# First two weight pairs of the down projection on the POOL queue, first pair's sums in the row ring

## The chip, the cores and the metric

One core of a Trainium2 chip. The metric is the device time of one execution in microseconds, median of several runs. TensorE (PE) multiplies, VectorE (DVE) and ScalarE (ACT) work on rows in SBUF and empty TensorE's banks, POOL (GpSimd) and SP (SyncE) here mainly issue DMAs, each on a queue of its own.

## The reference

One layer of a hybrid decoder on 1024 prompt tokens, 32 sample tokens and 16 meta tokens, in fp32: a norm, an input projection, a gated short convolution beside retention, an output projection, a second norm and a SwiGLU FFN. What matters here is its end:

```python
x = x + jnp.concatenate([conv_out, ret_out], axis=-1) @ w_out
xn = _rmsnorm(x, norm2_g)
x = x + (jax.nn.silu(xn @ w_gate) * (xn @ w_up)) @ w_down
...
y_prompt = _rmsnorm(xp, final_norm_g)[:, N_META:]
y_sample = _rmsnorm(xs, final_norm_g)
```

`w_gate` and `w_up` are 1024 x 2816, `w_down` is 2816 x 1024. A layer's `x` before the FFN is called `x1` below.

## The kernel before

**Numbers.** Every fp32 operand is split into two parts of a type that TensorE takes at full rate: hi (ScalarE, L153 for weights, L786 for FFN results) and lo = operand - hi (VectorE, L155, L787). Each product is made of three passes: hi by hi, hi by lo, lo by hi.

**Strassen.** The FFN's products and the down projection use a Strassen-Winograd scheme (`strassen`, L746) over 2 x 2 blocks: seven products instead of eight, in the order y1, z1, y2, w1, y3, z2, y4, into three PSUM banks `y`, `z` and `u` (names with the prefix "b" in the FFN, "d" in the down projection: `dy`, `dz`, `dw`). Four weight blocks a11, a21, a22, a12 are loaded into `wraw` (five buffers, `load_w`, L146, on SP's queue). Four sums of weights, s3 = a11 + a21, s1 = a21 + a22, s2 = s1 + a11, s4 = s2 + a12, are formed on VectorE (L750, names `s`); y1 needs a11 alone, z1 needs s3, y2 needs s2, w1 a12, y3 s1, z2 a22, y4 s4. After each product `on(step, ps)` is called, which reads the bank; y2, y3 and y4 go on adding in the bank of y1, so each has to wait until `on` has read what stood there.

**FFN.** A loop over 22 tiles of 128 hidden columns (`f`). Its right operands, the normed rows in seven Strassen combinations, are the 56 tiles `comb`. They lie in the pool `rows`: one ring of 62 buffers of 128 x 544 that serves nearly every row of the kernel (`ut`, L130). The FFN's other tiles (`gt`, `up`, sums of weights, ...) lie in the pool `late`. The result of a tile, `up`, is sent to DRAM (`hd`, and `hp` for the last four tiles) as hi and lo by the spill of the next tile, by POOL's queue (L788, L789). In the last tile (`f == NFF - 1`) the first rows `x1` (4 buffers) and the 28 tiles of block 0 are pulled back from DRAM into the ring (`pull`, L831, on SP's queue), four after each product.

**Down projection.** `late` is closed (L918) and the pool `fin` opened in its place. The hidden rows are taken in four blocks (`DBLOCKS`, `bi`), and per block in four pairs of output rows (`m` = 0, 2, 4, 6; called pair 0, 2, 4, 6), each one a `strassen` call with sums of weights in `fin` (two buffers of `ws`). Pair 0 of block 0 has its `x1` rows in the ring; for pairs 2, 4 and 6 four rows each are loaded into `fin` in block 0 (L948). `on` adds the bank to the `x1` row (L954) and pulls the next block's tiles, one after each product in block 0, so seven a pair:

```python
for m in range(0, KT, 2):
    ...                                   # four load_w of w_down
    if bi == 0 and m > 0:
        ...                               # four loads of x1 (L948)
    def on(step, ps):
        ...
        V.tensor_tensor(x, x, ps, ALU.subtract if i else ALU.add)   # L954
        advance(ahead, step_n)
    strassen(fin, a11, a21, a22, a12, w, nk, dn_rhs, "d", on)
```

**Order.** The order of the instructions on an engine or queue is not quite that of the text. The framework runs the program through a timing of its own: what is ready and has its buffers goes, and among what is ready what stands earlier in the text goes first. Then each engine runs its list strictly in that order. So an instruction that waits holds up all behind it on its engine.

## Time and profile before

| What | Value |
|---|---|
| Median of 3 runs | 1222.28 us (1221.14 to 1223.32) |
| The profiled execution | 1221.89 us, span of its instructions 1220.0 us |
| Granted clock of TensorE, mean | 0.992 |
| PE busy | 1196.4 us (98%) |
| DVE busy | 845.1 us (69%) |
| ACT busy | 486.3 us (40%) |
| POOL busy | 122.3 us (10%) |
| DMA | 163.02 MB, mean 134 GB/s |

The profile lists instructions by line, engine and operation, with names of tiles (`out<-in`). All matmuls of the FFN and the down projection have line 762, so products are told apart by their banks. `hb` and `ht` are pulled tiles of hidden rows, `hd` and `hp` their place in DRAM, `x1d` that of the rows `x1`, `by`, `bz`, `bw` the banks of the FFN, `dy`, `dz`, `dw` those of the down projection. PE is matmuls, PEld the weight loads beside them; SPq and POOLq are DMA issues on those queues. Times in the traces are microseconds from the start of the span; the last FFN tile runs from about 942.3 to 962.6.

### The profile page before, as it was taken

The numbers are of one execution on the slowest core, as the hardware profiler recorded it, in microseconds if no ns is written. First come the engines' busy times: TensorE is split into PE (matmuls) and PEld (weight loads), VectorE is DVE, ScalarE is ACT, GpSimd is POOL, SyncE is SP. The second block draws the span as 40 slices with busy tenths as digits, with TensorE's granted clock in tenths as the row PEclk, the third lists the DMA queues.
The fourth block names the chain that finished last, engine by engine and source line by source line (L and its number), as shares of the span: only waits on it lengthen the run. The fifth ranks groups of instructions, "written<-read, shape, count | busy, mean of one in ns | idle before, by whom it ended". The sixth has DMA issues, their size and how long they took to land.

```text
span 1220.0 us, 24549 instructions
## 1 busy us (share of the span) xinstructions
PE 1196.4 (98%) x9769; PEld 1183.3 (97%) x9769; DVE 845.1 (69%) x1592; ACT 486.3 (40%) x932; POOL 122.3 (10%) x251
## 2 busy tenths in 40 slices
PE   8999999999999999999999999999999899999996
PEld 8999988999999999999999999999999899999996
DVE  5455466676554577868777877787776588886665
ACT  8246531121223366644444444444343322222353
POOL 0100121000000012102201220222021100000000
PEclk9999998999999999999999999999999999999998
DMA  6321311100111255525424542544353998964213
GB/s 232 96 81 35 87 36 44 36 27 27 48 37 53 89 171 183 168 77 176 159 81 169 177 148 82 177 150 156 101 186 114 396 348 286 314 221 161 74 38 106
DMA packets 82066, 163.02 MB, mean 134 GB/s; under 512 B 10701, under 2 KB 23776, under 8 KB 81952
## 3 DMA queue, kind: packets, MB, share of 16 engines
q1 hardware_dynamic: 67568, 114.57, 29.1%
q0 software_dynamic: 14384, 46.89, 10.6%
q8 instruction: 77, 1.26, 0.4%
q14 instruction: 37, 0.30, 0.1%
HBM read 113.15 MB, written 48.26 MB: 132 GB/s over the span
## 4 chain that ended last, share of the span: by engine, by line
PE 80%; issue 10%; DVE 4%; DMA 3%; POOL 2%; ACT 1%; SPq 0%; DVEq 0%; POOLq 0%; ACTq 0%
PE by L762 14%; PE dy L762 8%; PE bz L762 7%; PE po L180 6%; PE pk L180 4%; PE dz L762 4%; PE pc L180 4%; PE pd L995 4%; PE pv L180 4%; PE pq L180 4%; PE pg L180 4%; PE bw L762 3%; PE pb L180 3%; PE ph L180 3%; PE dw L762 2%
## 5 line engine op out<-in xcount | busy, mean ns | idle before, releaser
L153 ACT ACTIVATE whi<-wraw 128x512 fp32r<-128x512 f32 (+2 forms) x198 | 115.6, 584 | 289.9 <-issue 62.8
L155 DVE TENSOR_TENSOR wlo<-wraw,whi 128x512 fp32r<-128x512 f32 (+2 forms) x198 | 124.4, 629 | 56.4 <-ACT whi L153 56.3
L153 ACT ACTIVATE whi<-s 128x512 fp32r<-128x512 f32 (+2 forms) x152 | 83.6, 551 | 162.7 <-PE by L762 49.7
L762 PE MATMUL by<-t,whi 128*128 128x256 f32 (+1 forms) x704 | 131.1, 285 | 0.0
L762 PE MATMUL bz<-t,whi 128*128 128x256 f32 (+1 forms) x704 | 131.0, 285 | 0.0
L762 PE MATMUL by<-b,whi 128*128 128x256 f32 (+1 forms) x704 | 129.9, 284 | 0.6 <-DVE up L890 0.6
L155 DVE TENSOR_TENSOR wlo<-s,whi 128x512 fp32r<-128x512 f32 (+2 forms) x152 | 89.4, 588 | 36.2 <-ACT whi L153 35.8
L762 PEld LDWEIGHTS by<-b,whi 128*128 128x128 f32 x704 | 109.3, 188 | 1.0 <-DVE up L890 1.0
L762 PEld LDWEIGHTS by<-t,whi 128*128 128x128 f32 x704 | 109.4, 188 | 0.0
L762 PEld LDWEIGHTS bz<-t,whi 128*128 128x128 f32 x704 | 109.4, 188 | 0.0
L762 PE MATMUL by<-t,wlo 128*128 128x256 f32 (+1 forms) x352 | 100.2, 285 | 0.0
L762 PE MATMUL by<-b,wlo 128*128 128x256 f32 (+1 forms) x352 | 100.2, 285 | 0.0
L762 PE MATMUL bz<-t,wlo 128*128 128x256 f32 (+1 forms) x352 | 100.2, 285 | 0.0
L762 PEld LDWEIGHTS by<-t,wlo 128*128 128x128 f32 x352 | 66.6, 189 | 0.0
L762 PEld LDWEIGHTS bz<-t,wlo 128*128 128x128 f32 x352 | 66.3, 188 | 0.0
L762 PEld LDWEIGHTS by<-b,wlo 128*128 128x128 f32 x352 | 66.1, 188 | 0.0
L762 PE MATMUL bw<-b,whi 128*128 128x272 f32 (+1 forms) x352 | 65.6, 285 | 0.0
L954 DVE TENSOR_TENSOR x<-x,dy 128x528 f32<-128x528 f32 x64 | 45.0, 704 | 25.9 <-PE dy L762 24.9
L788 POOL DMA_DIRECT2D hd<-hh x63 | 34.1, 542 | 277.8 <-ACT hh L786 275.7
L762 PE MATMUL dz<-ht,whi 128*128 128x256 f32 (+1 forms) x288 | 55.1, 288 | 3.6 <-ACT whi L153 3.6
L762 PE MATMUL dy<-hb,whi 128*128 128x256 f32 (+1 forms) x288 | 53.3, 284 | 1.7 <-ACT whi L153 1.7
L762 PEld LDWEIGHTS bw<-b,whi 128*128 128x128 f32 x352 | 54.5, 188 | 0.0
(303 smaller groups left out, 3200.5 us busy)
## 6 DMA issues: line engine op xcount, KB each, us to landing
ht<-hd SPq DMA_DIRECT2D x72, 264.0 KB, 5.1
hd<-hh POOLq DMA_DIRECT2D x63, 264.0 KB, 3.4
hd<-hl POOLq DMA_DIRECT2D x63, 264.0 KB, 3.7
hb<-hd SPq DMA_DIRECT2D x54, 264.0 KB, 5.1
wraw<-w_in SPq DMA_DIRECT2D x54, 256.0 KB, 2.8
wraw<-w_gate SPq DMA_DIRECT2D x44, 256.0 KB, 2.9
wraw<-w_up SPq DMA_DIRECT2D x44, 256.0 KB, 2.8
wraw<-w_out SPq DMA_DIRECT2D x32, 256.0 KB, 3.0
```

Of the source, the lines that this page charges most:

```text
L153: S.activation(hi[:, :n], raw[:, :n], AF.Copy)
L155: V.tensor_tensor(lo[:, :n], raw[:, :n], hi.bitcast(F32)[:, :n], ALU.subtract)
L180: T.matmul(ps[:, g, :n], wt[:, sl], xk[part][:, g * n:(g + 1) * n], start=(first and i == 0), stop=(last and i == 2))
L762: T.matmul(out, wt[:, sl], rhs(s, k, key, part), start=(first and k == 0 and i == 0), stop=(k == kt - 1 and i == 2), skip_group_check=not ...
L788: G.dma_start(dst[0], hi.bitcast(F32)[:, :HT])
L954: V.tensor_tensor(x, x, ps, ALU.subtract if i else ALU.add)
L995: T.matmul(ps[:, 0, :n], wt[:, sl], hs[k][g][part][:, SO[s]:SO[s] + n], start=(k == 0 and i == 0), stop=(k == NPL - 1 and i == 2))
```

## The change

- `load_w` takes the engine whose queue issues the load. A new function `down_w` makes the four loads of a pair.
- Pair 0 of block 0: its four loads are issued on POOL's queue, and stand in the text in the last FFN tile, after its product z2. Pair 2 of block 0: its four loads stay where they were and go to POOL's queue. All others stay on SP's queue.
- The four sums of weights of pair 0 of block 0 are tiles of the ring `rows` and not of `fin`.

```diff
-        def load_w(ap, n):
+        def load_w(ap, n, eng=D):
             raw = wts.tile([P, 512], F32, tag="wraw", name="wraw", bufs=5)
-            D.dma_start(raw[:, :n], ap)
+            eng.dma_start(raw[:, :n], ap)
             return raw
...
             def total(nm, a, b):
-                x = pool.tile([P, 512], F32, tag="ws", name=nm, bufs=4 if n > 384 else 2)
+                if pool is rows:
+                    x = ut(nm)
+                else:
+                    x = pool.tile([P, 512], F32, tag="ws", name=nm, bufs=4 if n > 384 else 2)
                 V.tensor_tensor(x[:, :n], a[:, :n], b[:, :n], ALU.add)
                 return x
...
+        def down_w(bi, m, eng=D):
+            p0, p1 = DBLOCKS[bi]
+            w, at = (p1 - p0) * P, 2 * p0 * P
+            return [load_w(t["w_down"][m + i][:, a:a + w], w, eng)
+                    for i, a in ((0, at), (1, at), (1, at + w), (0, at + w))]
+
+        down_first = []
...
+                if f == NFF - 1 and step == "z2":
+                    down_first.extend(down_w(0, 0, G))
                 if f == 0 and step in ("y2", "w1"):
...
             for m in range(0, KT, 2):
                 w = nk * P
-                at = 2 * p0 * P
-                a11, a21 = (load_w(t["w_down"][m + i][:, at:at + w], w) for i in range(2))
-                a22, a12 = (load_w(t["w_down"][m + i][:, at + w:at + 2 * w], w) for i in (1, 0))
+                if bi == 0 and m == 0:
+                    a11, a21, a22, a12 = down_first
+                else:
+                    a11, a21, a22, a12 = down_w(bi, m, G if bi == 0 and m == 2 else D)
...
-                strassen(fin, a11, a21, a22, a12, w, nk, dn_rhs, "d", on)
+                strassen(rows if bi == 0 and m == 0 else fin, a11, a21, a22, a12, w, nk, dn_rhs, "d", on)
```

## The prediction

> **What bounds the kernel now.** I read the page's busy times, then the waits of TensorE, then the chain of waits and the timelines around the change, then the DMA queues there. First the page and the two waits of TensorE that lie in this place:

> ```profile
> PE 1196.4 (98%) x9769; PEld 1183.3 (97%) x9769; DVE 845.1 (69%) x1592; ACT 486.3 (40%) x932; POOL 122.3 (10%) x251
> PE dz L762 <- ACT whi L153: 3.6, 1, 3.6
> PE dy L762 <- ACT whi L153: 1.7, 1, 1.7
> ```

> TensorE is the bound: time is saved where it stands still or runs slowly, and lost only where it stands. Both waits are at the start of the down projection. From the view of stretches (columns: length; busy time of PE, PEld, DVE, ACT, POOL; granted clock; DMA share and GB/s):

> ```profile
> 962.62:967.84 5.22, 1.63 (x15) 1.42 (x13) 4.05 (x8) 2.23 (x4) 1.91 (x4) 0.95 1.06 399
> 967.84:970.65 2.81, 2.81 (x13) 2.81 (x13) 2.20 (x6) 1.03 (x3) 0.24 (x1) 0.50 1.03 394
> 970.65:976.50 5.85, 5.85 (x49) 5.81 (x48) 3.27 (x7) 1.25 (x3) 0.00 (x0) 0.99 1.05 386
> 976.50:978.41 1.91, 0.17 (x3) 0.04 (x1) 1.53 (x4) 0.42 (x1) 0.00 (x0) 1.00 1.01 355
> ```

> The first product of pair 0 (y1) runs, then TensorE idles 5.22 - 1.63 = 3.59 us, then the next product (z1) runs at half the granted clock (0.50): 2.81 us. Four products later it idles 1.74 us more, with the clock at 1.00. The chain and VectorE's timeline say why:

> ```profile
> 966.83 0.43 DVE s L750
> 967.37 0.42 ACT whi L153
> 969.27 7.58 DMA wraw<-w_down
> 976.88 0.44 DVE s L750
> 988.81 2.93 PE dy L762 x24
> 998.99 2.93 PE dy L762 x24
> 965.48 1.32 DVE L787 TENSOR_TENSOR hl<-up,hh 128x528 fp32r<-128x528 f32 x2
> 966.83 0.76 DVE L750 TENSOR_TENSOR s<-wraw 128x256 f32<-128x256 f32 x2
> 976.88 0.81 DVE L750 TENSOR_TENSOR s<-wraw 128x256 f32<-128x256 f32 x2 [2.04 <-DMA wraw<-w_down]
> 977.61 0.70 DVE L954 TENSOR_TENSOR x<-x,dy 128x528 f32<-128x528 f32 x1
> ```

> Stall one: s3, the weight sum of z1, is formed at 966.83, right behind the last reader of the FFN's pool (L787, 965.48 + 1.32 = 966.80), because its tile lies in `fin`, which takes that pool's memory. Stall two: VectorE stands at the sums of pair 2 until their weights land (969.27 + 7.58 = 976.85); behind them in its queue is the L954 that empties the bank `y` of pair 0, and TensorE may write that bank again only at 977.61 + 0.70. From 988.81 to 998.99 is one pair undisturbed: 10.18 us, 1.454 a product.

> What the two stalls cost together, from TensorE's timeline:

> ```profile
> 962.62 0.42 PE L762 MATMUL dy<-hb,whi 128*128 128x272 f32 x2
> 982.84 0.41 PE L762 MATMUL dy<-ht,whi 128*128 128x272 f32 x2
> ```

> Product y2 of pair 2, the tenth, starts at 982.84. Undisturbed it would start at 962.62 + 9 x 1.454 = 975.71. So 7.1 us are there to be had: 3.59 idle, 2.81 - 1.45 = 1.36 slow clock, 1.74 idle, 0.4 at the edges.

> **The change, part by part.**

> *Sums of pair 0 in the row ring.* They no longer wait for the FFN's pool. Their weights are there (last load 944.55 on SP, below), and the FFN's own sums show how far ahead such a sum is run if it has a place: s of the last tile at 917.77 for a tile that starts with the second half of the piece at 939.34. Four additions of 0.43 us move into VectorE's gaps before 962. Stall one goes, with its slow clock: -4.95 us.

> ```profile
> 917.77 0.68 DVE L750 TENSOR_TENSOR s<-wraw 128x512 f32<-128x512 f32 x1
> 939.34 5.85 PE by L762 x48
> ```

> The ring is not free. Of its 62 places 56 hold the FFN's operands, 4 the rows `x1`; 2 are left, for the spill's hh and hl. Two early sums take these two. Then the first pulls of block 0 (942.67, below) and the last spill share what y1 of the last tile frees: one place for 3 matmuls, 0.37 us. Two places are 0.7 us of later start at worst in the likely course; 0 if the sums run later. I take 0.4; the far end is a whole FFN product, 2.9 us (half of 5.85).

> *Pair 0's loads on POOL's queue.* Four issues leave SP and go to POOL. Their time is set by the `wraw` buffers, as before; POOL is past its own stores when the last one comes free. An issue on POOL is 0.54 us, so eight are 4.3 us on an engine with 10% busy, and what stands behind them there is the spill's four stores, which are read only in the last block. Zero; if POOL held pair 0's last load back 5 us, it would still be 12 us ahead of its product.

> ```profile
> 965.03 0.54 POOL L788 DMA_DIRECT2D hp<-hh  x1 [16.62 <-ACT hh L786]
> hp<-hh POOLq DMA_DIRECT2D x4, 264.0 KB, 5.3
> ```

> *Pair 2's loads on POOL's queue.* With the sums done early, pair 0's weight buffers come free about 957 to 966 and the loads go then, not behind SP's seven pulls of block 1. At the 5.3 us of POOL's stores here they land before 972, and VectorE's next sums need them about then. Stall two goes: -1.74 and the edges, 7.1 in all with stall one.

> *What is late next.* SP's queue and the DMA engines:

> ```profile
> 942.67 1.79 SPq L831 DMA_DIRECT2D hb<-hd  x4
> 944.55 0.44 SPq L148 DMA_DIRECT2D wraw<-w_down  x1
> 964.12 0.33 SPq L148 DMA_DIRECT2D wraw<-w_down  x1
> 964.90 2.25 SPq L831 DMA_DIRECT2D hb<-hd  x4
> 967.51 1.66 SPq L831 DMA_DIRECT2D ht<-hd  x3
> 969.27 2.95 SPq L148 DMA_DIRECT2D wraw<-w_down  x3
> 973.59 2.54 SPq L948 DMA_DIRECT2D x<-x1d  x4
> 980.55 2.94 SPq L148 DMA_DIRECT2D wraw<-w_down  x4
> x<-x1d SPq DMA_DIRECT2D x1, 264.0 KB, 4.6
> wraw<-w_down SPq DMA_DIRECT2D x1, 128.0 KB, 5.1
> 945.00:950.00 5.00, 5.00 (x43) 5.00 (x42) 2.10 (x3) 2.79 (x5) 1.08 (x2) 1.00 0.99 363
> 1005.00:1010.00 5.00, 5.00 (x43) 5.00 (x42) 3.77 (x8) 1.04 (x3) 0.00 (x0) 1.00 1.01 332
> 1010.00:1015.00 5.00, 5.00 (x44) 5.00 (x43) 4.49 (x11) 1.49 (x5) 0.00 (x0) 1.00 0.55 196
> ```

> (The two single DMA rows are the first `x1` load at 973.59 and the first weight load at 980.55.) Of the thirteen 5 us stretches from 945 to 1010, first and last shown, the DMA share is 0.94 or more in all: the DMA engines are full for 65 us, and only then fall to 0.55. 264 KB at the 399 GB/s of the first stretch above are 0.68 us. Pair 2's first `x1` row lands at 973.59 + 4.6 = 978.2. Ahead of it in the new order are the same bytes: block 0's 28 pulls, the spill's stores, seven pulls of block 1, pair 2's four weight loads. That these four come by another queue changes their turn, not their sum, and the stream cannot start sooner, as its first pulls wait for the ring (942.67). So `x1` again lands at 978.2, while y1 of pair 2 would now end at 962.62 + 8 x 1.454 = 974.3. L954 for y1 needs that row, and y2 writes the same bank: it can start at 978.2 + 0.70 + 0.1 = 979.0, against 975.7. Given back: 3.3 us. The gain at y2 is 982.84 - 979.0 = 3.8. The bounds: 0 given back if the `x1` loads overtake the seven pulls (7 x 0.68 = 4.8 us, more than the 3.3 needed); 4.3 if the stream slips by another 1 us.

> [...]

> Then pair 4's first weight lands at 980.55 + 5.1 = 985.65; with 0.42 + 0.42 of splitting it is ready at 986.5, and its product would start at 979.0 + 5 x 1.454 = 986.3. Also VectorE's queue has a split between two L954s behind the late `x1` rows. I put 0.4 us on both; 0 to 0.9 (985.65 + 0.84 + one L954 of 0.70, less 986.3). SP reaches pair 4's rows without the eight weight issues, so after that the stream has slack: a pair moves 7 x 0.68 + 4 x 0.68 + 4 x 0.34 = 8.8 us of DMA against 10.18 of TensorE.

> The clock: TensorE will stand 979.0 - 975.7 = 3.3 us in one piece. Rows: 3.59 us of idling brought 0.50, worth 1.36 us; 1.74 brought nothing. 3.3 is nearer to the former, but the clock fell there only at the end of the wait (0.95 over 5.22 us is 0.5 us at half clock), so I take 0 and keep 1.4. [...]

> **Sum.** -7.1 + 3.3 + 0.4 + 0.4 = -3.0 us. The profiled execution took 1221.89 us (span 1220.0), 0.39 under the median of 1222.28: 1218.9 by it, **1219.3** by the median.

> **Rivals**, all from 1222.28.

> Full recovery: the `x1` loads are put ahead of the pulls. For it: SP's queue is free of the four weight issues, and the FFN's pool is free at 966.8. Against: before, the pulls went first although emitted just ahead. -7.1: 1215.2. Chance 0.17.

> The stall moves: the wait at y2 reaches the 3.59 us that cost the clock before (+1.4), or the ring delays the stream by a full 0.7 and pair 4's weights the full 0.9. -3.8 + 1.4 = -2.4 down to -3.8 + 1.4 + 0.7 + 0.9 = -0.8: 1219.9 to 1221.5. For it: the row of 0.50. This also holds the case that the change does not do what it says, the sums finding a place only when y4 of the FFN frees one. Chance 0.36.

> Slower: ring starvation. Early sums hold places that the pulls of block 0 need; SP's queue is in order and the DMA engines are full for the next 65 us, so each us of a later start is one at `x1`. It decides from 3.8 us of later start (no gain), 6.3 us for slower by 0.2%; that is more than two FFN products (2 x 2.93). At three, 8.8 - 3.8 = 5 us: 1227.3. Against: 8 places come free with each product, and the sums are four. Chance 0.06.

> **How the numbers follow.** Forecast 0.41 (1217.3 to 1219.8). About 0.2% (2.4 us) is what can be told from no change here, so faster is 0.41 + 0.17 = 0.58, same 0.36, slower 0.06. The range takes in full recovery and the moved stall: 1215.2 to 1222.2.

> **What would show it.** The 3.59 us wait and the 0.50 clock gone; L750 of pair 0 before 962; w_down issues on POOL; L948 of pair 2 at 969 to 971 on SP but landing near 978; TensorE waiting about 3 us for VectorE's L954 at y2 of pair 2. I am wrong if L948 lands by 975 (then 7 us), if TensorE waits inside the last FFN tile, or if the pulls of block 0 start after 944.

## The result, and the profile after

The changed kernel is slower. Its median is 1224.97 us (1223.49 to 1227.31, 7 runs) against 1222.02 us (1220.86 to 1223.32, 7 runs) of the kernel before; the ratio is 1.0028, with an interval of 1.0017 to 1.0038. Ratios and intervals here and below are taken over the runs; they differ a little from the quotient of the two medians. The profiled execution took 1226.44 us, its span is 1224.6 us.

From the page after, the busy times:

```profile
PE 1199.5 (98%) x9769; PEld 1186.9 (97%) x9769; DVE 845.2 (69%) x1592; ACT 486.8 (40%) x932; POOL 126.1 (10%) x259
```

From the view of waits, those of TensorE in this place (product, the engine and tile that ended the wait; us in total, times, longest; "issue" means that the trace gives no releaser):

```profile
PE dy L765 <- issue: 3.8, 1, 3.8
PE dz L765 <- ACT whi L153: 3.5, 1, 3.5
```

Stall one (3.6 us before) is there with 3.5 us. Stall two was 1.7 us and is 3.8. TensorE has 3.1 us more of busy time for the same 9769 matmuls, so it also ran slower. The stretches of after, with the columns of those of before:

```profile
963.72:968.80 5.08, 1.63 (x14) 1.43 (x12) 4.13 (x8) 2.24 (x4) 1.76 (x4) 1.00 1.05 397
968.80:971.80 3.00, 2.98 (x13) 2.69 (x14) 2.00 (x6) 1.03 (x4) 1.67 (x4) 0.54 1.04 399
971.80:975.10 3.30, 3.30 (x25) 3.16 (x24) 1.04 (x2) 0.83 (x2) 0.31 (x1) 0.90 1.06 416
975.10:978.90 3.80, 0.06 (x1) 0.00 (x0) 1.48 (x4) 0.42 (x1) 0.00 (x0) 1.00 1.03 378
978.90:983.60 4.70, 4.62 (x25) 4.65 (x26) 2.74 (x6) 0.42 (x1) 0.00 (x0) 0.64 1.06 400
```

Now there are two idle stretches and a slow clock behind each: 0.54 behind the first, 0.64 behind the second. VectorE's timeline shows the cause of both (start, duration, line, operation, output<-input, count; in brackets the idle time before it and what ended that):

```profile
966.58 1.32 DVE L790 TENSOR_TENSOR hl<-up,hh 128x528 fp32r<-128x528 f32 x2
967.82 0.75 DVE L753 TENSOR_TENSOR s<-wraw 128x256 f32<-128x256 f32 x2
...
977.30 0.97 DVE L753 TENSOR_TENSOR s<-wraw 128x256 f32<-128x256 f32 x2 [4.24 <-DMA wraw<-w_down]
978.18 0.70 DVE L967 TENSOR_TENSOR x<-x,dy 128x528 f32<-128x528 f32 x1
...
979.13 0.70 DVE L967 TENSOR_TENSOR x<-x,dw 128x528 f32<-128x528 f32 x1
```

First, pair 0's sums (967.82) still run right behind the last `hl`, though they lie in the ring. Second, VectorE stands 4.24 us at two sums of pair 2, and the addition of y2 of pair 0 (978.18, L967; L954 before) is queued behind them. In the kernel before the two sums (976.88) stood behind the additions of y2 and w1 and ahead of that of y3 alone:

```profile
973.80 0.70 DVE L954 TENSOR_TENSOR x<-x,dw 128x528 f32<-128x528 f32 x1 [0.41 <-PE dw L762]
```

So y3 of pair 0 has no bank until 978.9, and before it was y4 that waited. The loads of pair 2 in POOL's timeline:

```profile
950.85 0.54 POOL L148 DMA_DIRECT2D wraw<-w_down  x1 [1.33 <-DVE wlo L155]
...
968.63 0.54 POOL L792 DMA_DIRECT2D hp<-hl  x1
969.16 1.07 POOL L148 DMA_DIRECT2D wraw<-w_down  x2
971.57 0.54 POOL L148 DMA_DIRECT2D wraw<-w_down  x1 [1.33 <-issue]
```

Only one went early. The second was issued at 969.16, behind the spill's stores, and the sums could start at 977.30; before, SP issued them from 969.27 and the sums started at 976.88. In the time of the traces the other queue brought them no earlier. Counted from y1 of pair 0, which starts 1.10 us later here (963.72 and 962.62), the sums start 0.7 us sooner (13.58 and 14.26 us behind it). But in VectorE's list they stand two additions further ahead.

The stage from the first product of pair 0 to the last of the down projection is 190.96 us before and 194.70 after. Of these 3.74 us, 2.1 are idle (3.8 - 1.7) and 1.6 the second slow clock: y3 and z2 of pair 0 take 4.51 us, where two products at 1.454 are 2.91. The rest nearly cancels.

```profile
978.98:983.49 4.51, 4.51 (x24) 4.51 (x25) 2.66 (x6) 0.42 (x1) 0.00 (x0) 0.62 1.05 397
```

What the type of the split operands (fp32r) is worth shows in the trace of before: a matmul of it with 256 columns took 0.117 us (six from 989.41 to 990.11), one of unsplit fp32 operands with 32 rows and 256 columns 0.53 us (L524: two, in four records, from 178.41 to 179.47), both at a granted clock of 1.00.

### The profile page after: what moved, and what is told of

Read it like the earlier page. It is cut to its first block, busy times and chain, and to the rows that moved or that the text cites. A ratio compares the mean times of both kernels' runs of the same rounds, so it can differ in the third digit from the quotient of the medians.

```text
span 1224.6 us, 24557 instructions
## 1 busy us (share of the span) xinstructions
PE 1199.5 (98%) x9769; PEld 1186.9 (97%) x9769; DVE 845.2 (69%) x1592; ACT 486.8 (40%) x932; POOL 126.1 (10%) x259
## 4 chain that ended last, share of the span: by engine, by line
PE 89%; issue 5%; DVE 3%; DMA 2%; POOL 1%; ACT 1%; SPq 0%; DVEq 0%; POOLq 0%; ACTq 0%
PE by L765 18%; PE bz L765 9%; PE dy L765 9%; PE po L180 7%; PE bw L765 5%; PE dz L765 4%; PE pk L180 4%; PE pc L180 4%; PE pv L180 4%; PE pq L180 4%; PE pg L180 4%; PE pd L1008 3%; PE pb L180 3%; PE ph L180 3%; PE dw L765 2%
## 5 line engine op out<-in xcount | busy, mean ns | idle before, releaser
L153 ACT ACTIVATE whi<-wraw 128x512 fp32r<-128x512 f32 (+2 forms) x198 | 115.7, 585 | 292.6 <-issue 64.4
L153 ACT ACTIVATE whi<-s 128x512 fp32r<-128x512 f32 (+2 forms) x152 | 83.6, 551 | 164.8 <-PE by L765 50.3
L967 DVE TENSOR_TENSOR x<-x,dy 128x528 f32<-128x528 f32 x64 | 45.1, 704 | 27.9 <-PE dy L765 27.0
L765 PE MATMUL dy<-ht,whi 128*128 128x256 f32 (+1 forms) x288 | 55.2, 289 | 3.8 <-issue 3.8
## 6 DMA issues: line engine op xcount, KB each, us to landing
ht<-hd SPq DMA_DIRECT2D x72, 264.0 KB, 5.3
hd<-hh POOLq DMA_DIRECT2D x63, 264.0 KB, 3.5
hd<-hl POOLq DMA_DIRECT2D x63, 264.0 KB, 3.9
hb<-hd SPq DMA_DIRECT2D x54, 264.0 KB, 5.0
```

The source lines that it names most:

```text
L153: S.activation(hi[:, :n], raw[:, :n], AF.Copy)
L765: T.matmul(out, wt[:, sl], rhs(s, k, key, part), start=(first and k == 0 and i == 0), stop=(k == kt - 1 and i == 2), skip_group_check=not ...
```

## The experiments

Theory A: the places of the ring are given out in the order of the text. In the text the sums stand behind block 0's 28 pulls and the last spill, so they get their places no sooner than before; the loss comes from pair 2's loads on POOL. Rival B: POOL brings pair 0's weights late. Rival C: ring places taken by the sums hold up the pulls.

**One part at a time.** The ring alone (all loads on SP):

```diff
-                    down_first.extend(down_w(0, 0, G))
+                    down_first.extend(down_w(0, 0, D))
...
-                    a11, a21, a22, a12 = down_w(bi, m, G if bi == 0 and m == 2 else D)
+                    a11, a21, a22, a12 = down_w(bi, m, D)
```

> The sums of pair 0 lie in the ring; all loads stay on SP's queue. Theory A (places of the ring are handed out in the order of the text, so the sums come behind the last spill's hl whatever memory they lie in): L753 of pair 0 starts within 0.1 us of the end of the second hl, TensorE waits about 3.5 us before z1 as before, and the time is that of the kernel before within 0.2%. Theory B (the sums are late because POOL brings pair 0's weights late): with the loads on SP the sums run before y4 of the last FFN tile ends, the wait before z1 is gone, about -5 us at z1.

Measured: 1220.79 us against 1221.64 us, ratio 0.9995 (0.9985 to 1.0006). TensorE waits 3.5 us ahead of z1, as before. Its VectorE:

```profile
966.03 1.32 DVE L790 TENSOR_TENSOR hl<-up,hh 128x528 fp32r<-128x528 f32 x2
967.27 0.75 DVE L753 TENSOR_TENSOR s<-wraw 128x256 f32<-128x256 f32 x2
```

No gain, no loss. The sums are late without POOL too, against B, and the ring costs nothing, against C.

Only pair 0's loads on POOL (sums in `fin`, pair 2 on SP):

```diff
-                strassen(rows if bi == 0 and m == 0 else fin, a11, a21, a22, a12, w, nk, dn_rhs, "d", on)
+                strassen(fin, a11, a21, a22, a12, w, nk, dn_rhs, "d", on)
...
-                    a11, a21, a22, a12 = down_w(bi, m, G if bi == 0 and m == 2 else D)
+                    a11, a21, a22, a12 = down_w(bi, m, D)
```

> Only pair 0's four loads go to POOL's queue; the sums lie in fin, pair 2's loads on SP. Theory A: their last load is issued where its buffer comes free, about 15 us ahead of use, so nothing moves: same within 0.2%, both waits of TensorE as before (3.6 and 1.7 us). Theory B: pair 0's weights land later than the end of the last hl, and the wait before z1 grows beyond 3.6 us.

Measured: 1221.1 us against 1221.64, 0.9998 (0.9988 to 1.0008). No change: nothing is lost by the way of pair 0's weights. (The second wait was 0.7 us, not 1.7 as expected.)

Only pair 2's loads on POOL (sums in `fin`, pair 0 on SP; the diff is the first of the lines above and `down_w(0, 0, D)`):

> Only pair 2's four loads go to POOL's queue; the sums lie in fin. Theory A: the slower time comes from here. The plan puts pair 2's first sum ahead of the L967 of y2 instead of that of y3, the load for it lands no earlier (DMA engines full), so VectorE holds up y3 and not y4: second wait of TensorE 3 to 4 us instead of 1.7, with or without a phase at half clock behind it; +1.5 to +4 us. Rival C (ring: early sums hold places and the pulls start late): same as before here, since no sum lies in the ring.

Measured: 1222.57 us (1217.98 to 1227.1) against 1221.64, 1.0008 (0.9994 to 1.0023): not told from no change, and the second wait, 2.3 us, is shorter than the 3 to 4 expected. Its trace shows half of what the changed kernel has, with one of pair 2's sums ahead of the addition of y2:

```profile
974.88 0.42 DVE L753 TENSOR_TENSOR s<-wraw 128x256 f32<-128x256 f32 x1 [3.12 <-DMA wraw<-w_down]
975.23 0.70 DVE L967 TENSOR_TENSOR x<-x,dy 128x528 f32<-128x528 f32 x1
```

And the changed kernel without that part (`down_w(bi, m, D)` for pair 2, all else as changed):

> The changed kernel with pair 2's four loads back on SP's queue; the ring for pair 0's sums and POOL for pair 0's loads stay. Theory A (the loss comes from pair 2's loads on POOL, which move its two sums ahead of the addition of y2 of pair 0 in VectorE's order): no loss, 1221 to 1222.2, ratio 0.999 to 1.001, no half clock at y3 of pair 0. Rival C (the sums in the ring, with pair 0 on POOL, hold up the pulls or the sums): 1224 to 1225.5 as the changed kernel.

Measured: 1221.72 us against 1221.51, 1.0001 (0.9988 to 1.0013). The loss is gone, and the sums of pair 2 are back behind the addition of w1:

```profile
973.91 0.70 DVE L967 TENSOR_TENSOR x<-x,dw 128x528 f32<-128x528 f32 x1 [0.41 <-PE dw L765]
...
976.56 0.80 DVE L753 TENSOR_TENSOR s<-wraw 128x256 f32<-128x256 f32 x2 [1.61 <-DMA wraw<-w_down]
977.27 0.70 DVE L967 TENSOR_TENSOR x<-x,dy 128x528 f32<-128x528 f32 x1
```

So pair 2's loads on POOL are needed for the loss. By themselves they do not show it for certain; with the other two parts they do.

**The sums where they were meant to be.** In the changed kernel, pair 0's loads are written behind y1 of the last FFN tile and the four additions behind its y2, so behind 12 of block 0's 28 pulls in the text:

```diff
-                if f == NFF - 1 and step == "z2":
-                    down_first.extend(down_w(0, 0, G))
...
+                if f == NFF - 1 and step == "y1":
+                    down_first.extend(down_w(0, 0, G))
+                if f == NFF - 1 and step == "y2":
+                    first_sums((DBLOCKS[0][1] - DBLOCKS[0][0]) * P)   # the four V.tensor_tensor, into ut(...)
```

> The changed kernel with the four sums written in the last FFN tile, behind the pulls of its product y2 (loads behind those of y1), so that their places come ahead of the later pulls and of the last spill. Theory A: L880 of pair 0 runs about 953, the wait of 3.5 us before z1 and the half clock behind it are gone; then pair 2's x1 rows, landing at about 978, set y2 of pair 2 (wait of about 3 us there): 2 to 4 us faster than the kernel before. Theory B: sums wait for the weights, no gain at z1. Rival C: the first pulls of block 0 start after 944.5 and TensorE waits for pulled tiles.

The sums ran 10.3 us ahead of y1 of pair 0 (951.02, y1 at 961.32) instead of 4.1 behind it (967.82, y1 at 963.72), and stall one went with its slow clock. That the place in the text decides is shown by this: in the changed kernel the last weight for these sums landed at 951.84 and VectorE idled four times for 1.27 us or more between 950 and 961, so neither held them back until 967.82. That it decides through the places of the ring is argued, since the edit moves loads and sums together and no trace shows a place. But the time is 1221.93 us against 1221.64, 1.0001 (0.9991 to 1.0012): the loss of the changed kernel is gone, and there is no gain. VectorE:

```profile
951.02 0.75 DVE L880 TENSOR_TENSOR s<-wraw 128x256 f32<-128x256 f32 x2
...
977.55 0.70 DVE L980 TENSOR_TENSOR x<-x,dy 128x528 f32<-128x528 f32 x1 [1.89 <-DMA x<-x1d]
```

TensorE's waits in this place:

```profile
PE dy L767 <- DVE x L980: 2.0, 1, 2.0
PE dy L767 <- DVE wlo L155: 1.8, 2, 0.9
```

And four stretches from y1 of pair 0 on, each the time of 84 matmuls of the trace, a pair's worth of seven products:

```profile
961.32:971.74 10.42, 10.42 (x86) 10.28 (x85) 9.52 (x19) 4.32 (x10) 2.70 (x5) 1.00 1.05 386
971.74:985.06 13.32, 10.90 (x86) 10.43 (x85) 7.46 (x14) 2.30 (x6) 0.00 (x0) 1.00 1.05 389
985.06:996.53 11.47, 10.76 (x87) 10.36 (x85) 8.28 (x17) 2.59 (x7) 0.00 (x0) 1.00 1.04 368
996.53:1007.90 11.37, 10.49 (x87) 10.27 (x86) 8.62 (x18) 2.71 (x7) 0.00 (x0) 1.00 0.95 324
```

The same four stretches in the kernel before:

```profile
962.62:979.94 17.32, 11.98 (x87) 11.61 (x85) 12.55 (x26) 5.35 (x12) 2.15 (x4) 0.90 1.04 381
979.94:990.12 10.18, 10.18 (x87) 10.18 (x86) 8.47 (x18) 2.63 (x7) 0.00 (x0) 1.00 1.03 364
990.12:1000.30 10.18, 10.18 (x87) 10.18 (x86) 8.26 (x18) 2.70 (x7) 0.00 (x0) 1.00 1.00 335
1000.30:1010.48 10.18, 10.18 (x87) 10.18 (x86) 8.50 (x18) 2.81 (x7) 0.00 (x0) 1.00 0.99 343
```

Pair 0 is 6.9 us shorter (17.32 - 10.42). Pairs 2, 4 and 6 give back 3.14, 1.29 and 1.19, so block 1 starts 1.28 us early, and of a stage of 190.77 us (190.96 before) 0.19 are left at the end. The last two columns suggest a reason. Length by rate, block 0 moves 17.2 MB before and 17.1 MB here; at the 399 GB/s of a full stretch that would be 43 us, an estimate, and four undisturbed pairs of TensorE are 40.7. With 47.86 us for block 0 the kernel before had the room; without its stalls there is little. Theory D from here on: in block 0 the DMA stream is full, so what counts is the turn in which `x1`, weights and pulls land.

The first and longest wait is of that kind: y2 of pair 2 waits 2.0 us for an addition that waits for `x1` (977.55 above). The waits behind it are not all. The two of 0.9 us on `wlo` stand at the start of pair 6 and of block 1. ScalarE and VectorE ahead of the first:

```profile
993.63 0.42 ACT L153 ACTIVATE whi<-wraw 128x256 fp32r<-128x256 f32 x1 [2.16 <-DMA wraw<-w_down]
...
996.73 0.70 DVE L980 TENSOR_TENSOR x<-x,dy 128x528 f32<-128x528 f32 x1 [0.79 <-DMA x<-x1d]
997.35 0.42 DVE L155 TENSOR_TENSOR wlo<-wraw,whi 128x256 fp32r<-128x256 f32 x1
```

The weight had landed by 993.63, but its `wlo` stands in VectorE's list behind the addition of y4 of pair 4, the last of that pair, and so runs at 997.35. This is the order of a list and not a late landing. The same wait of 0.88 us comes back in the next two runs and in the run with late pulls on SP; the kernel before and the thinned run with early sums do not have it.

**Does the queue matter then?** Early sums, all loads on SP (`D` for `G` in both places):

> The four sums of pair 0 run inside the last FFN tile, as in the run before it with both pairs' loads on POOL, but here all loads stay on SP's queue. Theory A with D (the places of the ring decide when the sums run; after that the full DMA engines set the pace of block 0, whichever queue issues): stall one is gone, the wait of 3.6 us for whi of dz with it, and the time is that of the run with POOL, ratio 0.998 to 1.001 to the kernel before. Rival P (the POOL queue brings pair 2's weights earlier, and that is worth something once the sums are early): here pair 2's sums wait for their weights behind SP's seven pulls, y1 of pair 2 is late by 2 to 3 us, 1223.5 to 1224.5.

Measured: 1221.05 us against 1221.51, 1.0006 (0.9992 to 1.0019). It makes no difference that can be told; most of rival P's range (ratio 1.0016 to 1.0025) lies outside the interval. (Its profiled run took 1223.93 us, as it has a slow clock in block 0; more on that in the last section.)

**Is it the wait for x1 alone?** The same, with the `x1` rows of pair 2 pulled into the ring behind y4's pulls of the last FFN tile:

```diff
+                if f == NFF - 1 and step == "y4":
+                    pull_x1()            # x1[i][g] = pull(x1d[i, g], "x1", F32) for i in 2, 3
...
-                if bi == 0 and m > 0:
+                if bi == 0 and m > 2:
```

> As the run with early sums and all loads on SP, and the four x1 rows of pair 2 are pulled into the ring behind y4's pulls in the last FFN tile, so ahead of block 1's pulls. Theory D (the DMA stream is full to the end of block 0 and sets when that block can end): the 3 us wait at y2 of pair 2 is gone or under 1 us, but the bytes are the same, the idles come later in block 0, and the time is 1219.5 to 1221.5 with a lead at the end of block 0 under 1.5 us. Rival W (the x1 wait alone cost the gain, the later idles followed from VectorE's order behind it): the lead of some 5 us lasts, 1216 to 1217.5.

Measured: 1222.14 us against 1221.51, 1.0009 (0.9997 to 1.002). Theory D's range missed by 0.6 us, and rival W's times are out. At the end of block 0 the lead is 2.35 us, more than the 1.5 expected, and at the end of the stage nothing of it is left (190.96 us). The wait at y2 of pair 2 went, and the next late thing is the weights of pair 4, for whose `whi` TensorE waits 2.6 us; here it is a landing, as theory D says. The stretch of pair 2 and that wait:

```profile
974.42:987.40 12.98, 10.35 (x87) 10.16 (x85) 8.39 (x18) 2.65 (x7) 0.00 (x0) 1.00 1.04 387
```

**Thin the stream.** Early sums, and block 1's `lo` tiles are not pulled: 14 transfers of 264 KB less in block 0, the products of block 1 run with the `hi` tile in their place. Fewer places of the ring are held, too.

```diff
-                        hs[key][-1].append(pull(hd[p, i, part], "h" + key))
+                        hs[key][-1].append(hs[key][-1][0] if b == 1 and part else pull(hd[p, i, part], "h" + key))
```

> Early sums with both pairs' loads on POOL, and the pulls of block 1 bring only the hi tile of each row (14 transfers of 264 KB instead of 28; the lo tile is replaced by the hi tile, so the products of block 1 run on other numbers in the same count). Only the DMA stream of block 0 is thinned. Theory D: the idles behind y2 of pair 2 go, the lead of early sums (about 4 products, 5.8 us) lasts to the end of block 0, 1215 to 1217. Rival W (VectorE's order and x1's turn set the pace, not the bytes): x1 of pair 2 still lands near 977, the lead is eroded as before, 1220.5 to 1222.

Measured: 1215.42 us (1214.04 to 1216.23, 5 runs) against 1221.51, 0.9956 (0.9942 to 0.997). The control is the same edit in the kernel before:

> The kernel before with block 1's pulls halved (hi tile in the place of the lo tile, products of block 1 on other numbers in the same count): the control of the thinned run with early sums. Theory D: a thin stream without early sums takes stall two away at most, stall one stays: 1219.5 to 1221. Rival (thinning alone explains the 1215.4 of the thinned run with early sums, the early sums give nothing): 1215 to 1217.

Measured: 1221.05 us against 1221.62, 0.9999 (0.9986 to 1.0011). Thinning alone and early sums alone show nothing beyond the noise; together they bring 0.44%. The four stretches of the thinned kernel with early sums:

```profile
962.76:973.15 10.39, 10.39 (x87) 10.25 (x85) 9.51 (x19) 4.32 (x10) 2.69 (x5) 1.00 1.04 383
973.15:985.23 12.08, 10.45 (x87) 10.28 (x85) 8.91 (x19) 3.15 (x8) 0.00 (x0) 1.00 1.03 379
985.23:995.41 10.18, 10.18 (x86) 10.18 (x85) 8.62 (x18) 2.92 (x7) 0.00 (x0) 1.00 0.80 267
995.41:1005.60 10.19, 10.19 (x86) 10.19 (x85) 8.76 (x18) 2.92 (x7) 0.00 (x0) 1.00 0.95 324
```

And the first two of the control:

```profile
959.92:977.41 17.49, 12.12 (x86) 11.74 (x85) 12.66 (x26) 5.36 (x12) 2.15 (x4) 0.90 1.00 373
977.41:987.59 10.18, 10.18 (x86) 10.18 (x85) 8.74 (x18) 2.93 (x7) 0.00 (x0) 1.00 0.93 312
```

One detail of the expectation missed: pair 2 still takes 12.08 us, with 1.6 us of waiting at its y2, since its `x1` row lands at 976.9. What goes is everything behind it: pairs 4 and 6 are undisturbed, where they took 11.47 and 11.37 us with the full stream. This does not tell bytes from order: with fewer pulls VectorE's list is another one too, and the waits on `wlo` are gone from it. No run here holds that list fixed. In the control, stall two stays with 1.8 us.

**Only the turn.** Nothing left out: block 1's pulls begin with pair 2, four for three products, so `x1` and the weights of pair 2 are no longer behind seven pulls.

```diff
-                    advance(ahead, step_n)
+                    advance(ahead, step_n if bi else 0 if m == 0 else 1 + (step in ("z1", "y3")) if m < 6 else 1 + (step in ("z1", "y2", "y3")))
```

> Early sums, all loads on SP, and block 1's 28 pulls begin with pair 2 (four for three products) instead of with pair 0 (one a product), so x1 and the weights of pair 2 go ahead of seven pulls. Nothing is left out. Theory D (what is short is the turn of x1 and the weights in a full DMA stream, 7 x 0.68 = 4.8 us): x1 of pair 2 lands by 974, the idle at its y2 goes, the lead of early sums lasts in good part to the end of block 0: 1216 to 1218.5. Rival E (the same bytes are still needed by the end of block 0, and block 1's last tiles now come late): the idles move to the end of block 0 or the first pair of block 1, 1220.5 to 1222.5.

Measured, with early sums and all loads on SP: 1219.29 us (1214.74 to 1220.52) against 1221.62, 0.9977 (0.9966 to 0.9988).

> The same with the loads of pairs 0 and 2 on POOL's queue. Theory D: as the run with all loads on SP, within 1 us of it, 1216 to 1219. Rival P (the POOL queue matters once the stream has been thinned at this place): 1.5 us or more apart, either way.

Measured, with the loads on POOL: 1218.09 us (1215.69 to 1220.72), 0.9976 (0.9964 to 0.9987). Both beat both kernels, and the queue again makes no difference that can be told. The median with SP is 0.8 us above the expected range. SP's queue in the run with SP:

```profile
965.68 0.33 SPq L836 DMA_DIRECT2D hb<-hd  x1
967.84 3.74 SPq L974 DMA_DIRECT2D x<-x1d  x4
```

And its four stretches:

```profile
961.71:972.10 10.39, 10.39 (x86) 10.25 (x85) 9.51 (x19) 4.32 (x10) 2.15 (x4) 1.00 1.04 376
972.10:982.29 10.19, 10.19 (x86) 10.19 (x85) 6.38 (x13) 2.31 (x6) 0.00 (x0) 1.00 1.03 367
982.29:993.35 11.06, 10.68 (x86) 10.35 (x85) 8.91 (x19) 2.59 (x7) 0.00 (x0) 1.00 1.04 382
993.35:1005.05 11.70, 10.65 (x86) 10.23 (x84) 8.74 (x19) 2.71 (x7) 0.00 (x0) 1.00 1.03 369
```

`x1` is issued 6.1 us behind y1 of pair 0 (967.84 and 961.71), behind one pull; with early sums alone it was 9.2 us (970.52 and 961.32), behind seven. The first row lands at 973.12, before 974 as expected, and pair 2 is undisturbed. Pairs 4 and 6 give back 0.9 and 1.5 us, 0.9 of it the wait on `wlo`; the DMA share is 1.03 or more in each of the four stretches. Block 0 takes 43.34 us, 4.5 less than before; 3.1 of these are left at the end of the stage (187.87 us).

> The kernel before with only block 1's pulls moved to pairs 2, 4 and 6; the sums of pair 0 stay in the pool after the FFN's. Theory D: stall one and its half clock stay, stall two (1.7 us) goes or shrinks, as pair 2's weights land some 4 us earlier: 1219.8 to 1220.8. Rival (the late pulls alone bring the gain, the early sums are not needed): 1217 to 1218.5.

Measured, in the kernel before, with only this edit: 1221.24 us against 1221.62, 0.9997 (0.9985 to 1.0009). Stall two is gone from its trace as theory D has it, though the time is 0.4 us above the range. As with thinning, the turn is worth something only once the sums are early.

## Why the prediction was wrong

Forecast 1219.3 us, range 1215.2 to 1222.2; measured 1224.97. By its own steps:

- **Sums of pair 0 in the row ring (-4.95).** Failed, and with it the sum. The step took "they have a place" for "they run early". I counted free places, not the order in which they are given out: a sum that stands in the text behind 28 pulls and the spill ran behind the spill's last `hl`, at 967.82 and not before 962. Where the sums were written earlier, stall one and its slow clock went, so the price was right (pair 0 shorter by 6.9 us with both stalls, 7.1 foreseen) and the condition wrong. The prediction had this case in "the stall moves", at 1219.9 to 1221.5, with no price for what follows from it.
- **Pair 2's loads on POOL (-1.74 and the edges).** Failed: it leaned on the step above. The sums ran late, so three of the four loads went at 969.16 to 971.57, and the sums of pair 2 started 0.7 us sooner behind y1 of pair 0 than with SP. What I did not price is that another queue changes the order of VectorE: two sums ahead of an addition on which a bank depends. That is +2.1 us of idle and +1.6 of slow clock.
- **The clock.** "3.3 us of idling, I take 0" was a choice between two rows, and the runs show that these two could not decide it. At that place, y2 of pair 2, TensorE stood 2.04 us with the loads on POOL and 1.85 us with all on SP. Behind the longer wait the clock stayed at 1.00, behind the shorter it was 0.50 for 6.83 us, which cost about 2.6 us (an estimate: 5.94 us for 28 matmuls of 1.454 / 12 us). In the changed kernel the second stall, of 3.8 us, cost 1.6 us of clock; the case was named (+1.4) for another wait.
- **Give-back at y2 of pair 2 (gain 3.8).** About right once the sums are early: y1's addition starts at 977.55, with `x1` foreseen at 978.2. The wait is 2.0 us and not 3.3, because TensorE's list there has w1 ahead of y2. With both done at 979.8, 18.5 us behind y1 of pair 0 and 23.1 before, the gain is 4.6 us.
- **"After that the stream has slack."** Failed, and it would have sunk the forecast even with early sums: of the 4.6 us, 1.28 are left at the end of block 0 and 0.19 at the end of the stage. 8.8 us of DMA a pair against 10.18 leaves out the backlog with which the stage begins: in the run with early sums 12 of block 0's pulls had not landed at y1 of pair 0, and the spill's four stores were still to come, 16 x 0.68 = 10.9 us. Four times 1.4 us of slack do not clear that, by this estimate. It also leaves out VectorE's order, which makes the two waits of 0.88 us. How the loss divides between the two is open.
- **Queue against queue.** Here the issuing queue by itself makes no difference that can be told: with early sums the ratios are 1.0001 (POOL) and 1.0006 (SP), with late pulls 0.9976 (POOL) and 0.9977 (SP). The loss of the changed kernel came through VectorE's order.
- **The slower rival** was ring starvation. It was the right sign for the wrong reason: the ring edit alone is 0.9995.

What stays open: why pair 2 on POOL alone puts only one sum ahead, and with the ring two, was not taken apart; the framework's own timing is the likely place. The runs of the changed kernel reach from 1223.49 to 1227.31; slow clocks of different length would fit, but only one run has a trace.

## What to carry to other kernels

A tile moved to a larger pool ran earlier here only once its request stood earlier in the text; look at where the allocation is written, not at how many places are free. Before counting a stall as gain, add up the bytes of the stage it stands in, with the backlog at its start, against the engine's time: a stall may be the room in which a full DMA stream catches up. When an engine waits, look whether its input had landed: if it had, the order of a list is at fault. And where two limits take turns, each edit alone shows nothing (0.9999, 0.9997, 1.0001 here), and only the pair shows the gain (0.9956, 0.9977).

## What was not expected of the hardware

In each of the eight profiles with a wait of 3.5 or 3.6 us ahead of z1, z1 is slow (2.7 to 3.0 us for 1.45), as are the products behind the wait of 3.8. That looks like a bound on the length of a wait, and behind the waits of 1.7, 2.0, 2.3 and 2.6 us the clock was 1.00. But with early sums and all loads on SP, a wait of 1.85 us had the slow clock behind it. That wait and what follows:

```profile
977.03:978.88 1.85, 0.00 (x1) 0.00 (x1) 0.71 (x1) 0.39 (x1) 0.00 (x0) 1.00 1.05 400
978.88:979.97 1.09, 1.09 (x8) 1.09 (x9) 1.04 (x2) 0.00 (x0) 0.00 (x0) 1.00 1.04 391
979.97:986.80 6.83, 5.94 (x28) 5.68 (x27) 2.02 (x3) 0.42 (x1) 0.00 (x0) 0.50 1.03 359
```

And behind the 2.6 us, in the run with `x1` in the ring:

```profile
987.40:998.13 10.73, 10.73 (x84) 10.38 (x85) 7.93 (x17) 2.60 (x7) 0.00 (x0) 1.00 1.03 363
```

```profile
976.56:979.97 3.41, 1.56 (x13) 1.36 (x12) 1.74 (x3) 0.42 (x1) 0.00 (x0) 1.00 1.05 398
...
974.33:977.74 3.41, 1.72 (x14) 1.75 (x15) 2.23 (x5) 0.05 (x1) 0.00 (x0) 1.00 1.02 370
```

So in this stage, over these traces, the slow clock goes with the time that TensorE stands still within one step; the border lies between 1.56 and 1.72 us of work, near half of the step. By this reading a wait of 3.5 us leaves at least 1.7 us of idle in one step (an estimate: half of 3.5), while with a wait of 2 us it depends on where it falls: 1.85 us had the slow clock behind it, 2.0 us had not. It holds for one stage only: at 189.10 the clock falls in the kernel before with TensorE busy for the whole step ahead (3.41 us from 185.69), and near the end of the run with the ring alone it falls behind a step with 2.13 us of work.
